# RWKV heads: the inverse's blocks doubled by products of 32 and 64 rows in place of masked products of 128

## The chip, the cores and the metric

The kernel runs on one core of a Trainium2 chip. The number that counts is the time of one execution on the device, in microseconds (us). Before the change the median of 3 runs is 2561.5 us, with 2560.05 and 2563.88 us as the lowest and the highest. Five engines of the core work side by side, each on its own queue: TensorE (PE, with its weight loads as PEld), VectorE (DVE), ScalarE (ACT), GpSimd (POOL) and SyncE (SP), which issues most of the transfers.

## What is computed

Two blocks follow each other on 256 tokens of width 2048. The second begins with an RWKV group of 16 heads of width 64, beside an attention group. The part of the reference that the change touches is the recurrence of a head:

```python
def step(state, inp):
    r_t, w_t, k_t, v_t, kk_t, a_t = inp
    sa = jnp.einsum('bhvk,bhk->bhv', state, -kk_t)
    state = (state * w_t[:, :, None, :]
             + sa[..., None] * (kk_t * a_t)[:, :, None, :]
             + v_t[..., None] * k_t[:, :, None, :])
    return state, jnp.einsum('bhvk,bhk->bhv', state, r_t)
```

The kernel does not step through the tokens. It takes the 256 tokens as two chunks of 128 and solves the recurrence of a chunk by the inverse of a triangular 128 x 128 matrix per head, one plus a strictly triangular matrix of scores.

## The kernel before

**Halves, chunks and head groups.** `rwkv_half(hf, ...)` does 8 heads at a time, for `hf` = 0 and 1. Inside it `heads4(hg)` takes a group of 4 heads, `hg` = 0 and 1, and goes through the two chunks, `t` = 0 and 1; the second chunk needs the state `s0` that the first leaves. `together` takes the two groups in turns, one `yield` each, so what follows comes twice in the program at each place: four times over `hf` and `t`, each with two groups of 4 heads.

**The inverse.** The scores `sa` are made first. The 32 x 32 blocks on the diagonal of all 16 matrices of a half are inverted together on VectorE, one row after another (lines 1408 to 1412, tile `inv`), then turned into `invt` and `invx`, two layouts of one inverse (lines 1417 and 1418). Then `heads4` spreads the four blocks of each of its heads over a 128 x 128 matrix with zeros beside them (`spread`, line 1433), once as `wt` and once as its transpose `xt`, and doubles the blocks twice, from 32 to 64 (`l` = 5) and from 64 to 128 (`l` = 6). Each doubling is a product of the scores with `xt` (`pz`, line 1451), a multiplication with a mask `lev` that keeps the blocks beside the diagonal pairs (`zt`, line 1453), a product with `wt` (`pw`, line 1457) and an addition to `wt` (line 1458). Before the second doubling `xt` is made anew by a transpose on TensorE (`px`, line 1445) and a copy on ScalarE (line 1447). All of these are whole 128 x 128 matrices, 4 to a tile of 512 columns.

**What stands around it.** After the doubling come `pk` (line 1462) with `rhs` (1464), the product with the inverse `pg` (1471) and its copy `ga` (1473), the scores `psr` with `sr` (1389, 1391), and the output `py` (1489, 1490). At `t` = 0 the new state `pst` follows (1501, 1502), with 8 copies `s` on ScalarE (1508). At `t` = 1 the correction of the state, `rh` (1484), comes in before `py`. After both chunks the output `y` is normalised (1525 to 1543), mostly on VectorE.

**The other work.** `project` streams weights: SP loads `wr` (line 159), ScalarE rounds it into `wh` (148), VectorE makes the rest `wl` (151, 154), and TensorE does three products of 512 columns each (lines 163 to 165). The order in which each engine gets its instructions is laid down when the program is built, by a scheduler that goes by data and buffers. In half 0 it has placed products of the next projections between the steps of `heads4`; in half 1 there are none, and the chains of the two groups stand alone. The tag `side` has 3 banks of PSUM, in which `pz`, `pw`, `px`, `pk`, `pg`, `psr` and `py` follow one another.

Of the kernel before, what the change touches and what calls it, by code (L numbers as in the profile page):

```python
# [12 lines left out]
AL = mybir.AluOpType  # L13
# [11 lines left out]
C_IDENT, C_LT, C_GT, C_ONES, C_BD32, C_LE, C_SEL2, C_SEL4, C_FREQ, C_SEL8, C_ID32, C_ALL = (  # L25
    0, 128, 256, 384, 512, 640, 768, 770, 772, 796, 828, 860)
# [28 lines left out]
def tile_kernel(ctx: ExitStack, tc: tile.TileContext, I: dict, out: bass.AP):  # L55
    nc = tc.nc
    V, S, G, PE = nc.vector, nc.scalar, nc.gpsimd, nc.tensor
# [25 lines left out]
    def tl(tag, shape=None, dt=F, name=None):  # L83
        pool, (n, bufs) = (sb, BASE[tag]) if tag in BASE else (phase[1], phase[2][tag])
        shape = [128, n] if shape is None else shape
        return pool.tile(shape, dt, name=name or tag, tag=tag, bufs=bufs)
# [4 lines left out]
    def psum(tag, shape=None, name=None):  # L91
        return phase[3].tile(shape or [128, 512], F, name=name or tag, tag=tag, bufs=phase[4][tag])
# [4 lines left out]
    def pside(shape=None, name="side"):  # L97
        return psum("side", shape, name)
# [4 lines left out]
    def const(shape, name, dt=F):  # L103
        return sb.tile(shape, dt, name=name, bufs=1)
# [3 lines left out]
    cst = const([128, C_ALL], "cst")  # L108
    nc.sync.dma_start(cst[:, :128], I["cst"][:, :128])
    ident = cst[:, C_IDENT:C_IDENT + 128]  # L110
# [361 lines left out]
    for g in range(4):  # L472
        m = tl("g", [128, 2, 512], name="mem")
# [92 lines left out]
    lev = const([128, 7 * 128], "lev", U8)  # L566
# [39 lines left out]
    for d in range(2):  # L606
        for half in range(2):
            w = gate_w(d, half)
            la = []
            for t in range(2):  # L610
                px = pside()
# [18 lines left out]
            for q in (0, 2):  # L630
                pst = pside([128, 2, 256], name="pst")
                for r in range(2):
                    h = half * 2 + (q + r) // 2
# [261 lines left out]
    for p in range(2):  # L895
# [12 lines left out]
        for q in (0, 2):  # L908
            pt = transpose2(lambda t, kt: of[:, t, kt * 128:(kt + 1) * 128], q)
            h, l = ybT.h[p][:, q:q + 2], ybT.l[p][:, q:q + 2]  # L910
# [296 lines left out]
    bc4 = lambda m: m[:, None, :].to_broadcast([128, 4, 128])  # L1207
# [61 lines left out]
    def rwkv_half(hf, kx, rx, vx):  # L1269
# [6 lines left out]
        for dst, p0, b0 in ((sgm, 0, W0), (av, 64, A0)):  # L1276
            for q in (0, 2):
                pd = pside([128, 2, T], name="pd")
                for r in range(2):
                    PE.matmul(pd[:, r], wup[p0:p0 + 64, (q + r) * 128:(q + r + 1) * 128], lora[p0:p0 + 64, 0],  # L1280
                              start=True, stop=True)
                for r in range(2):
                    c = b0 + hf * 4 + q + r
# [19 lines left out]
        for q in (0, 2):  # L1303
            sq = tl("m", [128, 2, T], name="ksq")
            S.activation(sq, kk[:, q:q + 2], AF.Square)
            for r in range(2):
                c = C_SEL8 + (q + r) * 8
# [20 lines left out]
        for q in (0, 2):  # L1328
            fa = tl("m", [128, 2, T], name="fa")
            for r in range(2):  # L1330
                c = hf * 4 + q + r
# [3 lines left out]
            for r in range(2):  # L1335
                c = RK + hf * 4 + q + r
                V.scalar_tensor_tensor(qq[:, r], rx[:, q + r], pr3[:, c:c + 1], kx[:, q + r], op0=AL.mult, op1=AL.mult)
                c = C_SEL8 + (q + r) * 8
# [60 lines left out]
        for t in range(2):  # L1399
            for hg in range(2):  # L1400
                sa = sas[t, hg] = tl("g" if hf else "xt", [128, 2, 2, 2, 128], name="sa")
                scores(lambda o: sa[:, o], kk, strict, hg, t, "sa")
                b0 = (t * 2 + hg) * 4
# [12 lines left out]
        invx = tl("g", [128, 32, 32], name="invx")  # L1416
# [5 lines left out]
        def heads4(hg):  # L1422
            s0 = None
            for t in range(2):
# [3 lines left out]
                nt_ = lambda i: sa[:, i % 2, 0, i // 2]  # L1428
                b0 = (t * 2 + hg) * 4

                def spread(x, name):
                    d = tl("m", [128, 4, 128], name=name)
                    V.tensor_tensor(wide(d), x[:, :, b0:b0 + 4].rearrange("p i h -> p h i")[:, :, None, :].to_broadcast([128, 4, 4, 32]),
                                    wide(bc4(cst[:, C_BD32:C_BD32 + 128])), op=AL.mult)
                    return d


                wt = spread(invt, "wt")
                xt = spread(invx, "xt")
                for l in range(5, 7):  # L1440
                    yield
                    if l == 6:
                        px = pside([128, 4, 128], name="px")
                        for i in range(4):
                            PE.transpose(px[:, i], wt[:, i], ident)
                        xt = tl("m", [128, 4, 128], name="xt")
                        S.copy(xt, px)
                        yield
                    pz = pside([128, 4, 128], name="pz")
                    for i in range(4):  # L1450
                        PE.matmul(pz[:, i], nt_(i), xt[:, i], start=True, stop=True)  # L1451
                    zt = tl("m", [128, 4, 128], name="zt")
                    V.tensor_tensor(zt, pz, bc4(lev[:, l * 128:(l + 1) * 128]), op=AL.mult)
                    yield
                    pw = pside([128, 4, 128], name="pw")
                    for i in range(4):
                        PE.matmul(pw[:, i], zt[:, i], wt[:, i], start=True, stop=True)  # L1457
                    V.tensor_tensor(wt, pw, wt, op=AL.add)
                yield
                pk = pside([128, 4, 64], name="pk")  # L1460
                for i in range(4):
# [15 lines left out]
                if t:  # L1477
                    yield
                    pr_ = pside([128, 2, 128], name="pr_")
                    for i in range(4):  # L1480
                        c, o = divmod(i, 2)
# [5 lines left out]
                for i in range(4):  # L1487
                    c, o = divmod(i, 2)
                    PE.matmul(py[:, i], sr[o][:, 0, c], ga[:, i, :64], start=True, stop=False)
                    PE.matmul(py[:, i], sr[o][:, 1, c], vn[:, t, hg * 256 + i * 64:hg * 256 + i * 64 + 64], start=False,  # L1490
                              stop=t == 0)
# [3 lines left out]
                if t == 0:  # L1495
                    yield
                    pst = pside([128, 2, 64], name="pst")
                    for i in range(4):
                        c, o = divmod(i, 2)
# [10 lines left out]
        for _ in together(*[heads4(hg) for hg in range(2)]):  # L1510
            pass
# [221 lines left out]
    for hf in range(2):  # L1733
        for q in (0, 2):
            pt = transpose2(lambda t, kt: yr[hf][:, t, kt * 128:(kt + 1) * 128], q)
            h, l = yrT.h[hf][:, q:q + 2], yrT.l[hf][:, q:q + 2]
# [176 lines left out]
```

## Time and profile before

| | us |
|---|---|
| median of 3 runs | 2561.5 |
| lowest, highest | 2560.05, 2563.88 |
| the profiled execution | 2557.92 |
| its span in the trace | 2556.2 |
| PE busy in it | 2422.8 (95%) |
| DVE busy | 1796.2 (70%) |
| ACT busy | 1170.2 (46%) |

An engine counts as busy from the start of an instruction to its end, and those of TensorE overlap: a row of several products counts the whole stretch. The granted clock is given as a share of full speed, 1.00 for 2.4 GHz and 0.50 for 1.2 GHz. In the timeline a row may merge several instructions of one line (x16); each f32 product of the program leaves two records there, for `pz` 128 records for 64 products.

### The profile page before, as it was taken

To read this page: it belongs to the slowest core of one execution; us is meant where nothing else is said; L and a number is where in the kernel's file an instruction comes from. 1 tells how busy PE (TensorE), PEld (TensorE's weight loads), DVE (VectorE), ACT (ScalarE), POOL (GpSimd) and SP (SyncE) were. 2 spreads that over 40 slices of the span, in tenths; PEclk is the share of its full clock that TensorE was granted. 3 is DMA by queue.
4 is the path that set the end of the run, shared out by engine and by line. 5 is a ranking of instruction groups with operands and counts; after the bars stand their busy time and mean duration, and the time that the engine had idled before them with its cause. 6 is when DMAs were issued, how large, how long until landed. Compare 5 with 4: busy or idle time off the path is not lost.

```text
span 2556.2 us, 32427 instructions
## 1 busy us (share of the span) xinstructions
PE 2422.8 (95%) x11491; PEld 1928.6 (75%) x11491; DVE 1796.2 (70%) x2991; ACT 1170.2 (46%) x1560; POOL 172.1 (7%) x169
## 2 busy tenths in 40 slices
PE   8999998889989998998999999999999999999998
PEld 5667766778767776787878677787888888888886
DVE  5898657997897888967687978755655544555544
ACT  6543244444653544445642452445544433444433
POOL 0000010220230010002020120100000000000000
PEclk9999999999999999999999999999999999999999
DMA  7877547676656788755633243145466555666554
GB/s 262 276 251 225 170 153 242 218 232 228 198 183 218 233 282 288 259 182 158 198 94 110 80 136 99 63 163 192 133 189 182 186 187 187 189 184 187 201 188 154
DMA packets 267358, 483.11 MB, mean 189 GB/s; under 512 B 21137, under 2 KB 45547, under 8 KB 267195
## 3 DMA queue, kind: packets, MB, share of 16 engines
q1 hardware_dynamic: 266875, 480.60, 58.4%
q8 instruction: 90, 1.47, 0.2%
q14 instruction: 73, 0.60, 0.1%
q10 hardware_dynamic: 320, 0.44, 0.1%
HBM read 477.82 MB, written 3.15 MB: 188 GB/s over the span
## 4 chain that ended last, share of the span: by engine, by line
PE 61%; DVE 18%; DMA 11%; issue 6%; ACT 3%; POOL 1%; SPq 0%; DVEq 0%; ACTq 0%; POOLq 0%
PE acc L165 17%; PE acc L164 17%; PE acc L163 17%; DMA ar<-in_w_ada 8%; DVE wl L154 6%; DVE aa L405 3%; PE trp L236 2%; ACT wh L148 1%; DMA lnb<-in_ln_b 1%; PE pw L1457 1%; PE pz L1451 1%; DVE u L1411 1%; DVE inv L1412 1%; DMA wr<-in_w_in_e 1%; DMA wr<-in_w_in_o 0%
## 5 line engine op out<-in xcount | busy, mean ns | idle before, releaser
L148 ACT CAST wh<-wr 128x1024 fp32r<-128x1024 f32 (+2 forms) x736 | 760.3, 1038 | 991.6 <-PE acc L165 804.6
L164 PE MATMUL acc<-wl,xh 128*128 128x512 f32 (+2 forms) x2560 | 1005.5, 393 | 22.9 <-DVE wl L154 22.7
L163 PE MATMUL acc<-wh,xh 128*128 128x512 f32 (+2 forms) x2560 | 1011.8, 396 | 14.1 <-ACT xh L253 6.1
L165 PE MATMUL acc<-wh,xl 128*128 128x512 f32 (+2 forms) x2560 | 1003.5, 393 | 2.4 <-DVE xl L254 1.9
L154 DVE TENSOR_TENSOR wl<-wr,wh 128x512 fp32r<-128x512 f32 (+2 forms) x928 | 622.3, 702 | 176.8 <-ACT wh L148 176.1
L164 PEld LDWEIGHTS acc<-wl,xh 128*128 128x128 f32 x2560 | 485.1, 189 | 135.8 <-DVE wl L154 37.2
L151 DVE TENSOR_TENSOR wl<-wr,wh 128x1024 fp32r<-128x1024 f32 x272 | 333.3, 1225 | 357.4 <-ACT wh L148 355.4
L163 PEld LDWEIGHTS acc<-wh,xh 128*128 128x128 f32 x2560 | 484.6, 189 | 127.1 <-ACT wh L148 10.0
L165 PEld LDWEIGHTS acc<-wh,xl 128*128 128x128 f32 x2560 | 484.8, 189 | 106.3 <-issue 4.0
L405 DVE SCALAR_TENSOR_TENSOR aa<-ar,cs,aa 128x512 f32<-128x512 f32 x240 | 191.0, 796 | 72.8 <-DMA ar<-in_w_ada 71.5
L165 PE MATMUL acc<-wh,ucl 128*128 128x512 f32 x128 | 50.9, 398 | 0.0
L164 PE MATMUL acc<-wl,uch 128*128 128x512 f32 x128 | 50.7, 396 | 0.0
L163 PE MATMUL acc<-wh,uch 128*128 128x512 f32 x128 | 49.8, 389 | 0.0
L381 DVE SCALAR_TENSOR_TENSOR am<-ar,cs,am 128x512 f32<-128x512 f32 x60 | 42.6, 746 | 7.3 <-DMA ar<-in_w_ada 7.3
L722 PE MATMUL pp<-eq,ek 128*128 128x128 f32 x224 | 29.4, 286 | 6.1 <-DVE ek L734 6.1
L722 PEld LDWEIGHTS pp<-eq,ek 128*128 128x128 f32 x224 | 28.5, 201 | 8.4 <-issue 5.0
L1055 POOL TENSOR_TENSOR sgo<-sgo,psc 128x512 f32<-128x512 f32 x8 | 14.6, 1850 | 295.5 <-ACT sgo L1049 164.8
L350 PE MATMUL ada<-wl,c 128*4 128x512 f32 x64 | 26.0, 406 | 4.2 <-DVE wl L154 4.2
L164 PE MATMUL acc<-wl,dh 128*128 128x512 f32 x64 | 26.2, 410 | 3.8 <-DVE wl L154 3.7
L457 DVE SCALAR_TENSOR_TENSOR xl<-trp,pr,xh 128x256 fp32r<-128x256 f32 x48 | 22.3, 480 | 10.1 <-ACT xh L456 9.9
L1866 ACT ACTIVATE un<-acc,rml 128x512 f32<-128x512 f32 x32 | 22.0, 689 | 15.6 <-PE acc L165 15.6
L163 PEld LDWEIGHTS acc<-wh,uch 128*128 128x128 f32 x128 | 24.4, 191 | 5.6
(592 smaller groups left out, 2457.3 us busy)
## 6 DMA issues: line engine op xcount, KB each, us to landing
ar<-in_w_ada SPq DMA_DIRECT2D x288, 256.0 KB
wr<-in_w_in_e SPq DMA_DIRECT2D x128, 512.0 KB
wr<-in_w_up SPq DMA_DIRECT2D x128, 512.0 KB
wr<-in_w_down SPq DMA_DIRECT2D x128, 512.0 KB
wr<-in_w_in SPq DMA_DIRECT2D x80, 512.0 KB
wr<-in_w_in_o SPq DMA_DIRECT2D x64, 512.0 KB
wr<-in_w_ada SPq DMA_DIRECT2D x64, 256.0 KB
wr<-in_w_out_e SPq DMA_DIRECT2D x32, 512.0 KB
```

The costliest lines, as they stand in the source:

```text
L148: S.copy(wh, wr)
L151: engines[0].tensor_tensor(wl, wr, wh.bitcast(F), op=AL.subtract)
L154: engines[q % 2].tensor_tensor(wl[:, q], wr[:, q], wh[:, q].bitcast(F), op=AL.subtract)
L163: PE.matmul(acc, xh, wh, start=start, stop=False)
L164: PE.matmul(acc, xh, wl, start=False, stop=False)
L165: PE.matmul(acc, xl, wh, start=False, stop=stop)
L236: PE.transpose(pt[:, q, t * 128:(t + 1) * 128], src(t, kt + q), ident)
L350: PE.matmul(acc, c4[:, k0 + q], wl[:, q], start=False, stop=k0 + q == 15)
L381: V.scalar_tensor_tensor(acc[a], w[:, q], col, acc[a], op0=AL.mult, op1=AL.add)
L405: V.scalar_tensor_tensor(acc, w, cs[:, k:k + 1], acc, op0=AL.mult, op1=AL.add)
L722: PE.matmul(pp[:, h, t], kx[:, 2 * h + c, s * 128:(s + 1) * 128], qx[:, 2 * h + c, t * 128:(t + 1) * 128], start=c == 0, stop=c == 1)
L1411: V.tensor_tensor(u, inv[:, j + 1:, j:j + 1].to_broadcast([128, n, j]), inv[:, j:j + 1, :j].to_broadcast([128, n, j]), op=AL.mult)
```

## The change

`xt` as a whole matrix, the masks, the additions and the transpose `px` go. The first doubling takes the 32 x 32 blocks: `pz` multiplies the scores' block beside a diagonal pair with the block of `invx` itself, for the blocks 0 and 2 (8 products of 32 x 32 for 4 heads). The two results are copied to `zt` by VectorE and by ScalarE. `pw` then makes the two blocks beside the diagonal (8 products), which ScalarE copies into `wt`, and a third product for the transposed upper pair, which VectorE copies into `x6`, a 64 x 64 layout of the first pair that VectorE has spread from `invx`. The second doubling takes one block of 64 x 64 per head: `pzz` (4 products), a copy by VectorE (`zzt`), `pww` (4 products) and a copy by ScalarE into `wt`. That is 28 small products for 4 heads in place of 16 products and 4 transposes of 128 x 128.

```diff
@@ -1436,26 +1436,40 @@
 
 
                 wt = spread(invt, "wt")
-                xt = spread(invx, "xt")
-                for l in range(5, 7):
-                    yield
-                    if l == 6:
-                        px = pside([128, 4, 128], name="px")
-                        for i in range(4):
-                            PE.transpose(px[:, i], wt[:, i], ident)
-                        xt = tl("m", [128, 4, 128], name="xt")
-                        S.copy(xt, px)
-                        yield
-                    pz = pside([128, 4, 128], name="pz")
-                    for i in range(4):
-                        PE.matmul(pz[:, i], nt_(i), xt[:, i], start=True, stop=True)
-                    zt = tl("m", [128, 4, 128], name="zt")
-                    V.tensor_tensor(zt, pz, bc4(lev[:, l * 128:(l + 1) * 128]), op=AL.mult)
-                    yield
-                    pw = pside([128, 4, 128], name="pw")
-                    for i in range(4):
-                        PE.matmul(pw[:, i], zt[:, i], wt[:, i], start=True, stop=True)
-                    V.tensor_tensor(wt, pw, wt, op=AL.add)
+                x6 = tl("m", [128, 4, 64], name="x6")
+                V.tensor_tensor(x6[:64].rearrange("p h (g c) -> p h g c", c=32),
+                                invx[:64, :, b0:b0 + 4].rearrange("p i h -> p h i")[:, :, None, :].to_broadcast([64, 4, 2, 32]),
+                                cst[:64, C_BD32:C_BD32 + 64].rearrange("p (g c) -> p g c", c=32)[:, None].to_broadcast([64, 4, 2, 32]),
+                                op=AL.mult)
+                rows32 = [slice(g * 32, g * 32 + 32) for g in range(4)]
+                pz = pside([128, 4, 32], name="pz")
+                for i in range(4):
+                    for g in (0, 2):
+                        PE.matmul(pz[rows32[g + 1], i], nt_(i)[rows32[g], rows32[g + 1]], invx[rows32[g], :, b0 + i],
+                                  start=True, stop=True)
+                zt = tl("m", [128, 4, 32], name="zt")
+                for g in (1, 3):
+                    (V.tensor_copy if g == 1 else S.copy)(zt[rows32[g]], pz[rows32[g]])
+                yield
+                pw = pside([128, 2, 4, 32], name="pw")
+                for i in range(4):
+                    for g in (0, 2):
+                        PE.matmul(pw[rows32[g], 0, i], zt[rows32[g + 1], i], wt[rows32[g + 1], i, rows32[g + 1]], start=True, stop=True)
+                    PE.matmul(pw[rows32[1], 1, i], wt[rows32[1], i, rows32[1]], zt[rows32[1], i], start=True, stop=True)
+                V.tensor_copy(x6[rows32[1], :, :32], pw[rows32[1], 1])
+                for g in (0, 2):
+                    S.copy(wt[rows32[g], :, rows32[g + 1]], pw[rows32[g], 0])
+                yield
+                pz = pside([128, 4, 64], name="pzz")
+                for i in range(4):
+                    PE.matmul(pz[64:, i], nt_(i)[:64, 64:], x6[:64, i], start=True, stop=True)
+                zt = tl("m", [128, 4, 64], name="zzt")
+                V.tensor_copy(zt[64:], pz[64:])
+                yield
+                pw = pside([128, 4, 64], name="pww")
+                for i in range(4):
+                    PE.matmul(pw[:64, i], zt[64:, i], wt[64:, i, 64:], start=True, stop=True)
+                S.copy(wt[:64, :, 64:], pw[:64])
                 yield
                 pk = pside([128, 4, 64], name="pk")
                 for i in range(4):
```

The lines behind the change stand 14 higher: `pk` is line 1476, `rhs` 1478, `pg` 1485, `ga` 1487, `s` 1522.

VectorE, half 1, first chunk, from the turned inverse to `rhs`; before, `wt` and `xt` for each of the two groups stand first:

```order
L1418 STREAM_TRANSPOSE invx<-inv 128x1024
L1433 TENSOR_TENSOR wt<-invt,cst 128x512
L1433 TENSOR_TENSOR xt<-invx,cst 128x512
L1433 TENSOR_TENSOR wt<-invt,cst 128x512
L1433 TENSOR_TENSOR xt<-invx,cst 128x512
L1453 TENSOR_TENSOR zt<-pz,lev 128x512 x2
L1458 TENSOR_TENSOR wt<-pw,wt 128x512 x2
L1453 TENSOR_TENSOR zt<-pz,lev 128x512 x2
L1458 TENSOR_TENSOR wt<-pw,wt 128x512 x2
L1464 COPY rhs<-pk 128x4x64 x2
```

And now (`x_13077` and `x_13093` are `x6` of the two groups):

```order
L1418 STREAM_TRANSPOSE invx<-inv 128x1024
L1433 TENSOR_TENSOR wt<-invt,cst 128x512
L1440 TENSOR_TENSOR x_13077<-invx,cst 64x256
L1452 COPY zt<-pz 32x128
L1433 TENSOR_TENSOR wt<-invt,cst 128x512
L1440 TENSOR_TENSOR x_13093<-invx,cst 64x256
L1452 COPY zt<-pz 32x128
L1459 COPY x_13077<-pw 32x4x32
L1459 COPY x_13093<-pw 32x4x32
L1467 COPY zzt<-pzz 64x256 x2
L1478 COPY rhs<-pk 128x4x64 x2
```

The second group's `wt` now stands behind the first group's `zt`, which waits for TensorE, and eight multiplications or additions of 512 columns have become six copies of 128 or 256.

ScalarE, half 1, from the end of the first chunk into the second (`s_13202`, `s_13221` and later `s_13250`, `s_13281` are the states of the two groups). Before:

```order
L1473 COPY ga<-pg 128x4x64 x2
L1494 COPY y<-py 128x256 x2
L1508 ACTIVATE s_13202<-pst,fs 64x64 x4
L1508 ACTIVATE s_13221<-pst,fs 64x64 x4
L1447 COPY xt<-px 128x512 x2
L1473 COPY ga<-pg 128x512 x2
```

And now:

```order
L1487 COPY ga<-pg 128x4x64 x2
L1508 COPY y<-py 128x256 x2
L1522 ACTIVATE s_13250<-pst,fs 64x64 x4
L1452 COPY zt<-pz 32x128
L1522 ACTIVATE s_13281<-pst,fs 64x64 x4
L1452 COPY zt<-pz 32x128
L1461 COPY wt<-pw 32x4x32 x4
L1472 COPY wt<-pww 64x4x64 x2
L1487 COPY ga<-pg 128x512 x2
```

ScalarE's share of the first doubling stands behind the states of the first chunk. Each of its copies of `zt` also waits for VectorE's copy of the same tile.

TensorE, half 0, first chunk, the second doubling among the products of a projection. Before:

```order
L1445 MATMUL px<-cst,wt 128x128 x8
L163 MATMUL acc<-wh,xh 128x512
L164 MATMUL acc<-wl,xh 128x512
L165 MATMUL acc<-wh,xl 128x512
L1451 MATMUL pz<-xt,sa 128x128 x8
L1457 MATMUL pw<-wt,zt 128x128 x8
L1462 MATMUL pk<-vn,sa 128x64 x8
```

And now (`x_11030` and `x_11046` are `x6`):

```order
L1465 MATMUL pzz<-x_11030,sa 64x64 x4
L165 MATMUL acc<-wh,xl 128x512
L163 MATMUL acc<-wh,xh 128x512
L1465 MATMUL pzz<-x_11046,sa 64x64 x4
L164 MATMUL acc<-wl,xh 128x512
L165 MATMUL acc<-wh,xl 128x512
L1471 MATMUL pww<-wt,zzt 64x64 x8
L1476 MATMUL pk<-vn,sa 128x64 x8
```

Products of 512 columns now stand between small ones at more places. From the first `pz` to `pk` there were 9 of them in the first chunk and, from `pst` on, 5 in the second; now there are 12 and 9. In half 1 none stands there, before or after. SP's and POOL's queues keep their order.

## Rows read from the trace of the kernel before

**Rows 1.** The page, busy time and chain: engine, us, share, instructions.

```profile
PE 2422.8 (95%) x11491; PEld 1928.6 (75%) x11491; DVE 1796.2 (70%) x2991; ACT 1170.2 (46%) x1560; POOL 172.1 (7%) x169
PE acc L165 17%; PE acc L164 17%; PE acc L163 17%; DMA ar<-in_w_ada 8%; DVE wl L154 6%; DVE aa L405 3%; PE trp L236 2%; ACT wh L148 1%; DMA lnb<-in_ln_b 1%; PE pw L1457 1%; PE pz L1451 1%; DVE u L1411 1%; DVE inv L1412 1%; DMA wr<-in_w_in_e 1%; DMA wr<-in_w_in_o 0%
```

**Rows 2.** Windows around half 1: length, PE, PEld, DVE, ACT, POOL busy, PEclk, DMA.

```profile
1570.00:1580.00 10.00, 6.01 (x33) 5.87 (x34) 7.79 (x9) 0.00 (x0) 0.00 (x0) 0.66 0.12 45
1580.00:1590.00 10.00, 9.76 (x92) 9.41 (x92) 4.31 (x7) 1.92 (x4) 0.00 (x0) 1.00 0.00 0
1640.00:1660.00 20.00, 19.71 (x118) 16.38 (x117) 14.86 (x42) 12.96 (x30) 0.00 (x0) 1.00 0.44 146
```

**Rows 3.** Timeline, half 1, first chunk: start us, us, engine, line, operation.

```profile
1570.16 1.86 DVE L1418 STREAM_TRANSPOSE invx<-inv 128x1024 f32<-128x1024 f32 x1
1571.95 0.97 DVE L1433 TENSOR_TENSOR wt<-invt,cst 128x512 f32<-128x512 f32 x1
...
1573.99 3.91 PE L1451 MATMUL pz<-xt,sa 128*128 128x128 f32 x16 [4.89 <-DVE xt L1433]
...
1585.13 1.90 PE L1462 MATMUL pk<-vn,sa 128*128 128x64 f32 x16
```

**Rows 4.** Timeline, half 1, second chunk.

```profile
1595.56 0.34 PE L1501 MATMUL pst<-ga,bn 128*64 128x64 f32 x4
...
1596.39 2.57 ACT L1508 ACTIVATE s<-pst,fs 64x64 f32<-64x64 f32 x8 [0.35 <-PE pst L1502]
...
1606.30 1.90 PE L1462 MATMUL pk<-vn,sa 128*128 128x64 f32 x16
```

**Rows 5.** Timeline, half 0, both chunks.

```profile
1359.40 2.00 DVE L1418 STREAM_TRANSPOSE invx<-inv 128x1024 f32<-128x1024 f32 x1
...
1375.63 1.90 PE L1462 MATMUL pk<-vn,sa 128*128 128x64 f32 x16
...
1386.75 0.34 PE L1501 MATMUL pst<-ga,bn 128*64 128x64 f32 x4
...
1398.07 1.90 PE L1462 MATMUL pk<-vn,sa 128*128 128x64 f32 x16
```

**Rows 6.** Timeline, half 1: weight loads of products of several shapes, and two copies on VectorE.

```profile
1581.24 1.92 PEld L1451 LDWEIGHTS pz<-xt,sa 128*128 128x128 f32 x16
...
1586.17 0.42 DVE L1464 COPY rhs<-pk 128x256 f32<-128x256 f32 x1
...
1588.74 0.52 PEld L1389 LDWEIGHTS psr<-rr,av 64*128 64x128 f32 x8
...
1589.18 0.53 PEld L1389 LDWEIGHTS psr<-rr,rk 64*128 64x128 f32 x8
...
1594.96 0.30 PEld L1489 LDWEIGHTS py<-ga,sr 128*128 128x128 f32 x2
...
1595.18 0.30 PEld L1490 LDWEIGHTS py<-vn,sr 128*128 128x128 f32 x2
...
1595.55 0.20 PEld L1501 LDWEIGHTS pst<-ga,bn 128*64 128x64 f32 x4
...
1596.37 0.25 PEld L1502 LDWEIGHTS pst<-vn,kn 128*64 128x64 f32 x4
...
1598.49 0.16 DVE L1526 TENSOR_SCALAR ymean<-ymean 128x8 f32<-128x8 f32 x1
```

**Rows 7.** Timeline, a projection ahead of half 1.

```profile
1563.09 0.39 PE L165 MATMUL acc<-wh,xl 128*128 128x512 f32 x1
...
1563.54 0.39 PE L164 MATMUL acc<-wl,xh 128*128 128x512 f32 x1
```

**Rows 8.** Windows of 1 and 2 us, columns as in rows 2: where the clock was low.

```profile
158.00:159.00 1.00, 1.00 (x8) 0.88 (x7) 0.95 (x4) 0.34 (x1) 0.00 (x0) 0.77 0.85 319
1576.00:1578.00 2.00, 2.00 (x11) 2.00 (x11) 0.75 (x2) 0.00 (x0) 0.00 (x0) 0.50 0.00 0
1580.00:1582.00 2.00, 1.76 (x15) 1.51 (x15) 0.69 (x1) 1.03 (x2) 0.00 (x0) 1.00 0.00 0
```

**Rows 9.** Timeline of TensorE just ahead of the first window of rows 8.

```profile
157.26 1.15 PE L356 MATMUL pm<-cst,m 4*128 4x128 f32 x8 [0.79 <-DVE m L353]
158.34 0.97 PE L236 MATMUL trp<-cst,xn 128*128 128x128 f32 x4
```

## The prediction

> **What bounds the kernel now.** I read the page first. TensorE is busy for 95% of the span, and the chain that ended last runs 17% each through the three products of the projections; the doublings `pz` and `pw` stand in it with 1% each, some 50 us together [rows 1]. So the kernel as a whole is bound by TensorE's projections, and the question is what bounds the four stretches in which the inverses are doubled. The windows around half 1 tell that: no transfer to speak of from 1570 us on, VectorE busy for 4.3 us of 10 and ScalarE for 1.9 [rows 2]. TensorE counts 9.8 of 10, but no projection stands there: it works through the chain's own products, one stage after the other, each handed to VectorE and back. Whatever shortens a stage there shortens the whole. From 1640 us on TensorE is full again with projections [rows 2] and stays so; its work there does not change, so time saved in a chain is not given back later.
>
> I measure each chain to the first `pk`, since everything from there on is as before. In half 1 the first chunk's chain starts when VectorE ends `invx`, at 1570.16 + 1.86 = 1572.02, and `pk` starts at 1585.13: 13.1 us [rows 3]. For the second chunk I count from the first `pst`, 1595.56, to `pk` at 1606.30: 10.7 us [rows 4]. In half 0 it is 1361.40 to 1375.63, 14.2 us, and 1386.75 to 1398.07, 11.3 us [rows 5]; 9 and 5 products of projections stand in these two.
>
> **Prices.** A copy on VectorE took 0.42 us for 256 columns, an operation on 8 columns 0.16 [rows 6]; on that line 128 columns cost 0.29. The spread `wt` of 512 columns took 0.97 [rows 3], so `x6` with half the columns should take 0.5. An activation on ScalarE took 2.57/8 = 0.32 [rows 4]; I take that for each of its small copies. A product of 512 columns takes (1563.54 - 1563.09)/2 = 0.225 us [rows 7].
>
> No row shows a product of 32 x 32. Its price is bounded by the nearest ones. Each f32 product leaves two records. With weights of 128 columns a record takes 1.92/16 = 0.12 us; `psr`, with 64 rows, 0.44/8 = 0.055; `pst`, with weights of 64 columns, (1596.37 - 1595.55)/28 = 0.029 [rows 6]. So 0.029 to 0.12; nearest by shape is `pst`, then `psr`, and I take 0.04. A change of shape costs something too: from `py` to `pst` it is 0.37 us from load to load, where it is 0.22 from one pair of `py` to the next: 0.15 us [rows 6].
>
> This last row has a rule beside it. The Trainium skill, TensorEngine Tiling, section Key Properties, says that changing the tiling mode, not merely the tile, drains TensorE. The trace agrees with 0.15 us at the change from `py` to `pst`; were such changes free, as if that rule did not hold, the saving below would be 2.7 us larger.
>
> **The new chain, first chunk of half 1.** `pz` no longer waits for the spreads; it runs on `invx` itself while VectorE does `wt`, `x6`, `zt`, then the same for the second group: 2 x (0.97 + 0.5 + 0.29) = 3.5 us. `pz` (32 records, 1.3 us) and the first group's `pw` (24 records, 1.0 us) lie beside it. ScalarE's copy of the second `zt` waits for VectorE's: 0.32. Then on the path: `pw` of the second group, 24 records, `pzz` and `pww`, 8 each: 40 x 0.04 = 1.6; the copy to `x6` 0.3 and to `zzt` 0.42; the tail of the last record twice, 0.2 each, 0.4; five hand-overs of some 0.06 (an estimate), 0.3; two changes of shape (32 to 64, 64 to 128), 0.3. ScalarE's copies into `wt` lie beside `pzz`, and the last one beside `pk`, which hides it. Sum 3.52 + 0.32 + 3.32 = 7.2, against 13.1: 5.9 us less at full clock.
>
> **The clock.** At 1576 us TensorE runs at 0.50 of full speed, after standing idle while VectorE turned and spread the inverse; it is back at 1.00 in the window from 1580 [rows 8], after the dense 128-wide `pz` and `pw`. Now these are gone, and TensorE waits for most of the chain. I assume that the low clock lasts through the chain and into `pk` and `pg` behind it, and take 2.0 off: 40 records at twice the price are 1.6, the rest is for `pk`. The other end is 3.4, if `pk` and `pg` (3.7 us together) run low as well, or 0. **First chunk of half 1: 3.9 us less.**
>
> **Second chunk of half 1.** What is late here is ScalarE: its copies of `zt` stand behind the states of the first chunk. From `pst`: 16 records and a tail, 0.7; four activations, 1.3; `zt`, 0.32; four more, 1.3; `zt`, 0.32: 3.9 us, where VectorE's spreads and the mean of `y`, which now stand between its copies, are ready in time. Behind that the same as above, 40 records and so on: 3.3. Sum 7.2 against 10.7: **3.5 us less**. TensorE comes from dense `py` here, and I charge no low clock; the other end is 3.4.
>
> **Half 0.** The same two chains, with products of projections among them. First chunk: 7.2, plus 12 products, 2.7 us, of which half fills waits of the chain, 1.35; one `wl` on VectorE that stands before the second copy to `x6`, 0.68; ten changes of shape more, 1.5, half of them in waits, 0.75. Sum 10.0 against 14.2, and 3 products more than before are then done, 0.7: **4.9 us less**. Second chunk: 7.2 + 1.0 for half of 9 products + 0.75 = 9.0 against 11.3, and 4 products more, 0.9: **3.2 us less**.
>
> **Sum.** 3.9 + 3.5 + 4.9 + 3.2 = 15.5 us. The profiled execution would go from 2557.92 to 2542.4. It lies 3.6 below the median of the runs; the difference holds for the median, 2561.5 - 15.5 = 2546. The bounds: with records at 0.029 (1.8 more), no loss by the clock (2.0) and all products and changes of shape hidden (3.85), 23.2 us; with 0.055 (2.4 less), nothing hidden (3.85) and the low clock to its other ends (1.4 and 3.4), 4.5 us. What I count at nothing is VectorE's lighter work beyond the path (six small copies for eight operations of 512 columns): it has idle time in these chains. The changed order of other work around half 0's end I charge at nothing too, since the same instructions follow there.
>
> **The rivals.**
>
> *Small products are as dear as large ones.* The change makes 28 products of 16 products and 4 transposes. If a small record costs what a wide one does, 0.12 [rows 6], the chain goes by TensorE: 56 records of `pz` and the first `pw` with 0.5 of waits, 40 more behind, 1.7 of the rest: 13.7 us. The four chains then take 54.8 + 1.35 + 0.68 + 0.75 + 1.0 + 0.75 = 59.3 us against 49.3 + 1.6 for the products done meanwhile: 8.4 us more, 2570 us. It decides from 0.1 us per record on, where the chains are even. For it: both blocks of a `pz` go to one bank, where `psr` has a bank for each of its halves. Against it: `pst` writes one bank with two column groups at 0.029 [rows 6]. The Trainium skill, TensorEngine Tiling, section Gotcha 1: PSUM Pressure, says that different row tiles cannot access one PSUM bank at the same time; no row shows two row tiles at one bank, and by that rule the blocks 0 and 2 would take turns and a record would lie nearer to 0.055. Chance 7%.
>
> *The low clock takes it.* Ahead of 158 us TensorE was busy with products that use 4 rows of the array, and the granted clock was 0.77 of full speed right behind them [rows 8, 9]: products that fill little of the array may not keep it up. If each chain ends at half speed and leaves `pk` and what follows low for 3.4 us or more in half 1, with the dear ends of the other terms, about 4.5 us remain: 2557, within what can be told from no change. Chance 10%.
>
> *Half 0 gives nothing.* There TensorE always has projections to do [rows 5], and if the chain's idle time was filled anyway only half 1 counts: 7.4 us, 2554. Against it: TensorE's own work falls, from 72 wide records a pair of groups (8.6 us) to 112 small ones (4.5). Chance 12%.
>
> *More than forecast*: PE's waits vanish as the bound says and more, below 2538. Chance 5%.
>
> **How the numbers follow.** My forecast, 10 to 23 us less, has 66%; with half 0 giving nothing 12% and the larger gain 5%, faster by more than 0.2% (5.1 us, about what a measurement of this kernel tells from no change) has 83%; the low clock is the 10% for no change, the dear products the 7% for slower. The range from 2538 to 2557 takes in the bounds of 23.2 and 4.5 us, and leaves out the slower case, the larger gain and half of the low clock.
>
> **What would show it.** In the profile after, `pk` of half 1 should start some 9 us after `invx` ends and 7.2 us after the first `pst`. The loads of `pz` and `pw` should follow each other by 0.03 to 0.055 us. ScalarE's `zt` should follow the states, and TensorE's granted clock between `invx` and `pk` tells the second rival. I am wrong if a small record takes 0.1 us or more, if the second chunk waits for something else than ScalarE, or if the time from the end of the chains to the end of the kernel has grown.

## The result, and the profile after

The change makes the kernel slower: 2574.64 us as the median of 6 runs against 2562.69 for the kernel before beside it, a ratio of 1.0053 with a 95% interval of 1.0037 to 1.007. That is 12 us more, where I forecast 15.5 us less. In a later comparison the ratio was 1.0046 (last experiment). The profiled execution took 2572.85 us, its span is 2571.1.

Here is the page of the changed kernel, busy time by engine. TensorE has 160 more records of products and is busy 18 us longer than in [rows 1], though the products it got are smaller than those it lost.

```profile
PE 2441.1 (95%) x11651; PEld 1943.4 (76%) x11651; DVE 1777.4 (69%) x2983; ACT 1174.7 (46%) x1584; POOL 171.0 (7%) x169
```

The timeline of half 1 of the changed kernel, start and duration in us, from the turned inverse to the first `py` of the second chunk. It answers to [rows 3, 4].

```profile
1579.30 1.86 DVE L1418 STREAM_TRANSPOSE invx<-inv 128x1024 f32<-128x1024 f32 x1
...
1581.28 0.99 PEld L1448 LDWEIGHTS pz<-invx,sa 32*32 32x32 f32 x32 [3.48 <-issue]
...
1587.26 1.84 PEld L1471 LDWEIGHTS pww<-wt,zzt 64*64 64x64 f32 x16
...
1589.22 3.67 PE L1476 MATMUL pk<-vn,sa 128*128 128x64 f32 x16
1592.69 3.62 PE L1485 MATMUL pg<-rhs,wt 128*128 128x64 f32 x16
...
1608.11 0.49 PE L1515 MATMUL pst<-ga,bn 128*64 128x64 f32 x4
...
1609.39 1.27 ACT L1522 ACTIVATE s<-pst,fs 64x64 f32<-64x64 f32 x4 [0.80 <-PE pst L1516]
1610.68 0.26 ACT L1452 COPY zt<-pz 32x128 f32<-32x128 f32 x1
...
1616.83 3.67 PE L1476 MATMUL pk<-vn,sa 128*128 128x64 f32 x16
1620.29 3.73 PE L1485 MATMUL pg<-rhs,wt 128*128 128x128 f32 x16
...
1629.34 0.43 PE L1503 MATMUL py<-ga,sr 128*128 128x64 f32 x2
```

Read the starts. From the end of `invx` (1581.16) to `pk` it is 8.1 us, 13.1 before: the chain that the change shortens did get shorter. The 16 records of `pk`, untouched by the change, take 3.67 us in place of 1.90, and from `pk` to `pst` it is 18.9 us. The same rows of half 0, which answer to [rows 5]:

```profile
1361.58 1.90 DVE L1418 STREAM_TRANSPOSE invx<-inv 128x1024 f32<-128x1024 f32 x1
...
1375.64 3.67 PE L1476 MATMUL pk<-vn,sa 128*128 128x64 f32 x16
1379.07 0.77 PE L163 MATMUL acc<-wh,xh 128*128 128x512 f32 x1
1379.65 0.63 PE L164 MATMUL acc<-wl,xh 128*128 128x512 f32 x1
...
1396.24 0.49 PE L1515 MATMUL pst<-ga,bn 128*64 128x64 f32 x4
...
1405.89 2.00 PE L1476 MATMUL pk<-vn,sa 128*128 128x64 f32 x16
...
1416.23 0.43 PE L1503 MATMUL py<-ga,sr 128*128 128x64 f32 x2
```

Two rows of the kernel before close the comparison at the far end, the first `py` of the second chunk in half 0 and in half 1:

```profile
1407.85 0.43 PE L1489 MATMUL py<-ga,sr 128*128 128x64 f32 x2
...
1614.89 0.43 PE L1489 MATMUL py<-ga,sr 128*128 128x64 f32 x2
```

From these rows and [rows 3, 4, 5], each piece before and after, in us:

| piece | half 0 before | after | half 1 before | after |
|---|---|---|---|---|
| end of `invx` to `pk`, t = 0 | 14.2 | 12.2 | 13.1 | 8.1 |
| `pk` to `pst`, t = 0 | 11.1 | 20.6 | 10.4 | 18.9 |
| `pst` to `pk`, t = 1 | 11.3 | 9.7 | 10.7 | 8.7 |
| `pk` to `py`, t = 1 | 9.8 | 10.3 | 8.6 | 12.5 |

The four doubling chains became 10.8 us shorter together. What stands behind them, in which the change touches no instruction of the heads, became 22.4 us longer; in half 0 the order puts 11 products of projections there where there were 8, at 0.225 us each [rows 7] some 0.7 us of it. The balance is 11.6 us more, and the medians differ by 12. (The two profiled spans differ by 14.9; the other 3.3 us lie outside these stretches and are no more than executions of one kernel differ among themselves.)

The windows of the changed kernel say why. The columns are as in [rows 2]: length, busy time of PE, PEld, DVE, ACT, POOL, then the granted clock. First half 0, then half 1.

```profile
1366.00:1368.00 2.00, 2.00 (x25) 1.40 (x26) 1.73 (x5) 0.60 (x3) 0.00 (x0) 0.50 0.00 0
1384.00:1386.00 2.00, 2.00 (x18) 2.00 (x18) 0.00 (x0) 0.37 (x1) 0.00 (x0) 0.50 0.04 15
1398.00:1400.00 2.00, 2.00 (x18) 1.41 (x18) 1.93 (x3) 1.80 (x7) 0.45 (x1) 0.54 0.00 0
1400.00:1402.00 2.00, 2.00 (x53) 1.27 (x55) 1.23 (x5) 1.22 (x5) 0.40 (x1) 1.00 0.00 0
...
1580.00:1582.00 2.00, 0.69 (x25) 0.72 (x27) 2.00 (x3) 0.00 (x0) 0.00 (x0) 0.68 0.21 80
...
1590.00:1592.00 2.00, 2.00 (x11) 2.00 (x11) 0.42 (x1) 0.00 (x0) 0.00 (x0) 0.50 0.00 0
...
1618.00:1620.00 2.00, 2.00 (x11) 2.00 (x11) 0.42 (x1) 0.00 (x0) 0.00 (x0) 0.50 0.00 0
...
1624.00:1626.00 2.00, 2.00 (x22) 2.00 (x22) 0.32 (x1) 0.58 (x1) 0.00 (x0) 0.72 0.29 107
```

TensorE goes at half speed (1.2 in place of 2.4 GHz) from about 1366 to 1399 us and from about 1581 to 1625 us: 33 and 44 us, busy in most of the windows. In half 0 products of projections with 512 columns stand among the chain's own in this time, three in a row from 1379.07 us on (two of them are shown above), and the clock stays at 0.50 through them. In the kernel before it was back before `pk` in both halves, in half 1 by [rows 8]; for half 0 these are its windows, which I had not read:

```profile
1363.00:1365.00 2.00, 1.71 (x9) 1.72 (x9) 2.00 (x3) 0.00 (x0) 0.00 (x0) 0.61 0.01 3
1365.00:1367.00 2.00, 2.00 (x12) 1.95 (x10) 1.29 (x3) 0.00 (x0) 0.00 (x0) 0.54 0.00 0
1367.00:1369.00 2.00, 2.00 (x18) 1.91 (x17) 1.77 (x3) 0.00 (x0) 0.00 (x0) 1.00 0.00 0
```

### The profile page after: what moved, and what is told of

It is laid out like the page before. It is cut to its first block, busy times and chain, and to the rows that moved or that the text cites. A ratio compares the mean times of both kernels' runs of the same rounds, so it can differ in the third digit from the quotient of the medians.

```text
span 2571.1 us, 32754 instructions
## 1 busy us (share of the span) xinstructions
PE 2441.1 (95%) x11651; PEld 1943.4 (76%) x11651; DVE 1777.4 (69%) x2983; ACT 1174.7 (46%) x1584; POOL 171.0 (7%) x169
## 4 chain that ended last, share of the span: by engine, by line
PE 66%; DVE 16%; DMA 10%; issue 4%; ACT 3%; POOL 1%; SPq 0%; DVEq 0%; ACTq 0%; POOLq 0%
PE acc L165 18%; PE acc L164 18%; PE acc L163 18%; DMA ar<-in_w_ada 7%; DVE wl L154 5%; DVE aa L405 2%; PE trp L236 2%; ACT wh L148 1%; DMA wr<-in_w_in_o 1%; PE psr L1389 1%; DVE u L1411 1%; DVE inv L1412 1%; PE pk L1476 0%; DMA lnb<-in_ln_b 0%; PE pg L1485 0%
## 5 line engine op out<-in xcount | busy, mean ns | idle before, releaser
L163 PEld LDWEIGHTS acc<-wh,xh 128*128 128x128 f32 x2560 | 486.0, 190 | 128.7 <-ACT wh L148 11.3
L1055 POOL TENSOR_TENSOR sgo<-sgo,psc 128x512 f32<-128x512 f32 x8 | 13.9, 1752 | 293.1 <-ACT sgo L1049 164.8
```

The source lines that it names most:

```text
L163: PE.matmul(acc, xh, wh, start=start, stop=False)
```

## The experiments

Theory 1: the masked 128 x 128 products of the old doublings brought the clock back on their way; without them it stays low through `pk`, `pg`, `psr` and `py`, and that costs more than the chains gain. Theory 2, the rival: the small products, their hand-overs and their order are dear in themselves, and the clock is a bystander. Added products write to a tile of the tag `bg`, not to the three banks of `side`, and nothing reads it. The edits are shown shortened, some of them in words.

**One doubling of each kind.** The first run keeps the small first doubling and makes the second as before (transposes, product, mask, product, 128 wide); the second run the other way round.

```diff
 e1: first doubling small, then
-  pzz, zzt, pww of 64 rows
+  px (4 transposes), xt, pz 128x128, zt masked, pw 128x128, wt += pw
 e2: first doubling masked 128x128, then
+  px (4 transposes of 64x64), x6
   pzz, zzt, pww of 64 rows
```

> Only the first doubling is small; the second is the old round of masked 128x128 products (transposes, product, mask, product). Theory 1 (the clock): the time was lost because, after the idle time behind the transposed inverse, nothing but products of few moving columns follows and the clock stays at 0.50 through pk, pg, psr and py (pk to pst 20.6 us in half 0 and 18.9 us in half 1, before 11.1 and 10.4). The 12 dense 128-column products in front of pk bring it back: pk's 16 records about 1.9 to 2.5 us in place of 3.7, pk to pst 11 to 13 us at t = 0 in both halves, and the kernel about 2556 to 2563. Theory 2 (the small products and their hand-overs are dear in themselves): half of them is left, so about half of the 12 us lost, 2566 to 2570, with pk at 3.7 us as in the changed kernel.

> Only the second doubling is small (its transposed operand by four 64x64 transposes); the first is the old round of masked products. Theory 1: the 8 dense products come first, then 12 small ones with waits between them; the clock comes back partly, and falls or stays according to which comes last, so 2558 to 2568; pk's 16 records take 1.9 us where the granted clock is 1.00 in front of them and 3.7 us where it is 0.50, and the time of the kernel goes with that and not with the number of small products. Theory 2: about half of the loss, 2566 to 2570, whatever the clock.

Measured: 0.9988 of before (0.9971 to 1.0005) for the small first doubling, 1.0003 (0.9984 to 1.0022) for the small second. By the ratios the small first doubling alone is 17 us faster than both (1.0053 - 0.9988 of 2560): far more than the half of the loss that theory 2 gives back. The interval of the small second doubling reaches up to 1.0022, into that half, so its time alone does not decide. The stretches do: `pk` to `pst` is 11.1 and 10.4 us in one, 11.0 and 10.5 in the other, as before the change. Two rows of the first run, half 1:

```profile
1575.09 1.90 PE L1476 MATMUL pk<-vn,sa 128*128 128x64 f32 x16
...
1585.51 0.34 PE L1515 MATMUL pst<-ga,bn 128*64 128x64 f32 x4
```

The second run has more to show. In its half 1 the clock is at 1.00 behind the first chunk and then falls behind `pzz` and `pww` of the second chunk. Its TensorE timeline and its windows there:

```profile
1596.92 1.25 PE L1461 MATMUL pzz<-x,sa 64*64 64x64 f32 x16
1598.11 1.28 PE L1467 MATMUL pww<-wt,zzt 64*64 64x64 f32 x16
1599.33 3.67 PE L1472 MATMUL pk<-vn,sa 128*128 128x64 f32 x16
```

```profile
1596.00:1597.00 1.00, 0.56 (x8) 0.34 (x6) 0.52 (x1) 0.37 (x1) 0.00 (x0) 1.00 0.00 0
1597.00:1598.00 1.00, 1.00 (x16) 0.96 (x16) 0.37 (x1) 0.37 (x1) 0.00 (x0) 1.00 0.00 0
1598.00:1599.00 1.00, 1.00 (x16) 0.88 (x15) 0.48 (x2) 0.18 (x1) 0.00 (x0) 1.00 0.00 0
1599.00:1600.00 1.00, 1.00 (x10) 0.90 (x8) 0.00 (x0) 0.56 (x2) 0.00 (x0) 0.60 0.00 0
```

TensorE has hardly stood idle ahead of this fall: 0.44 us in the window from 1596 and, from 1587 us on, 0.14 us besides. From 1597 on it is busy throughout, with products of 64 x 64, and loses the clock all the same. `pk` takes 3.67 us, and from `pk` to `py` it is 11.9 us (8.6 before).

**The clock given back by extra products.** A burst ahead of `pk`, and products in the waits.

```diff
 e3, behind pww of the second group, t = 0
+  12 products of 512 columns
 e4, t = 0
+  2 f32 products of 512 columns on invt, ahead of the first pz
+  3 products of 512 columns behind pz, each pw, each pzz and the last pww
```

> The changed kernel with 12 extra products of 512 moving columns, whose results nothing uses, between the last small product and pk at t = 0 of both halves. Theory 1: they bring the clock back: pk 1.9 us, pk to pst 11 to 12 us (20.6 and 18.9 without); they cost 2.7 us each time at full clock, at most 5.4 us at 0.50, so the kernel gains 18 less 5 to 11: 2562 to 2569. Theory 2: pure extra work in the chain, 2575 plus 5 to 11: 2580 to 2586.

> The changed kernel with extra products of 512 moving columns, whose results nothing uses, put at t = 0 of both halves into the waits that TensorE has there anyway: 2 behind the transposed inverse in front of the first small product, 3 in each wait for a copy of a small product. Theory 1: the clock is back before pk at little cost, since TensorE was idle there: pk to pst 10.5 to 12 us in both halves, the chain ahead of pk at most 2 to 3 us longer: 2553 to 2562. Theory 2: the clock at pk changes nothing that matters: 2575 to 2582.

Measured: 1.0014 (0.9998 to 1.003) and 0.9978 (0.9956 to 1.0001). Both give TensorE further products and are, by the ratios, faster than the changed kernel by 10 and 19 us. Theory 2 called for 5 to 11 us more in the first and for no gain in the second, and it falls here. In the run with a burst `pk` to `pst` is back to 10.8 and 10.4 us. In the run with products in the waits the clock is 1.00 throughout half 0 and the first chunk of half 1. Its rows, half 1:

```profile
1570.82 1.14 PE L1487 MATMUL pww<-wt,zzt 64*64 64x64 f32 x16
1571.89 0.96 PE L1430 MATMUL warm<-xh 128*128 128x512 f32 x3
1572.68 1.89 PE L1494 MATMUL pk<-vn,sa 128*128 128x64 f32 x16
...
1590.47 3.67 PE L1494 MATMUL pk<-vn,sa 128*128 128x64 f32 x16
```

The first `pk` takes 1.89 us. The second, at t = 1, where no product was added, takes 3.67: the clock fell there too.

**Only the columns of `pk` and `pg`.** No product is added or moved; `pk`, and `pg` at t = 0, get their 64 moving columns twice.

```diff
-  PE.matmul(pk[:, i], sa[...], vn[:, t, h], ...)
+  PE.matmul(pk[:, i].rearrange("p (a b) -> p a b", a=2), sa[...],
+            vn[:, t, h][:, None, :].to_broadcast([128, 2, 64]), ...)
```

> The changed kernel with the same 64 moving columns given twice to pk, and to pg at t = 0, so that these products have 128 moving columns (the second 64 columns of the result are not used); no other product is added. Reading 1a (the clock came back in the kernel before because its products there had 128 moving columns, and stays away because pk and pg have 64): the clock returns within pk and pg of t = 0, psr and py go at full clock, pk to pst 15 to 17 us in place of 20.6 and 18.9, and the kernel 2562 to 2570. Reading 1b (the columns don't matter; the pauses ahead do): the clock stays at 0.50 to py as in the changed kernel, pk to pst 19 to 21 us, the kernel 2572 to 2578.

Measured: 0.9969 (0.9949 to 0.9988), some 21 us below the changed kernel and beyond what reading 1a called for. The timeline and the windows of half 1:

```profile
1576.12 3.78 PE L1476 MATMUL pk<-vn,sa 128*128 128x128 f32 x16
1579.69 2.10 PE L1489 MATMUL pg<-rhs,wt 128*128 128x128 f32 x16
...
1588.45 0.34 PE L1520 MATMUL pst<-ga,bn 128*64 128x64 f32 x4
```

```profile
1576.00:1578.00 2.00, 2.00 (x11) 1.88 (x10) 0.00 (x0) 0.37 (x1) 0.00 (x0) 0.50 0.03 8
1578.00:1580.00 2.00, 2.00 (x11) 2.00 (x11) 0.42 (x1) 0.00 (x0) 0.00 (x0) 0.50 0.00 0
1580.00:1582.00 2.00, 2.00 (x20) 1.88 (x21) 0.42 (x1) 0.55 (x2) 0.00 (x0) 1.00 0.00 0
```

`pk` starts at 0.50 as in the changed kernel and takes 3.78 us with twice the columns (3.67 with 64): at half speed these cost next to nothing. Then the clock is back, `pg` takes 2.10 us in place of 3.62, and `pk` to `pst` is 12.3 us (18.9). In half 0 it is 12.6 (20.6). TensorE was as busy by the profile in one as in the other; the columns of `pk` and `pg` are what the edit changes. The control is the same edit in the kernel before:

> The kernel before, with its full masked products, and the same wide pk and pg (128 moving columns at t = 0): the control for the changed kernel with wide pk and pg, which was 0.9969 of before. If those gain by the clock alone, there is nothing to gain here, since the clock is at 1.00 from before pk on: 2556 to 2562, ratio 0.999 to 1.001 (each set of 16 records is 0.05 to 0.15 us longer). If the wide products are a gain in themselves, 0.992 to 0.997.

Measured: 0.9992 (0.9974 to 1.0011). Where the clock is already up, the wide products gain nothing that can be told. So their gain in the changed kernel is the clock's.

**Extra products alone, fewer, and more.** Four f32 products in the old kernel's wait ahead of its first `pz`; the two of that place alone in the changed kernel; and the products in the waits also at t = 1 of half 1.

```diff
 e6 (kernel before) and e8 (changed kernel), behind invt
+  for _ in range(4):    # 2 in e8
+      PE.matmul(bank, ident, flat(invt)[:, :512], ...)
 e7 (as the products in the waits)
-  if t == 0 and hg in ...
+  if (t == 0 or hf) and hg in ...
```

> The kernel before, with its full masked products, and 4 extra products of 512 moving columns behind the transposed inverse, in the wait in front of the first pz (results not used). It tells how much of the gain of the small products with extra products in the waits is theirs, and how much the extra products alone give. Theory 1 (the clock decides, and at equal clock the small products are worth the 3 to 6 us per half that their shorter chains show): the first pz in half 1 goes at 2.2 us in place of 3.9, the chain to pk is about 3 us shorter, nothing else moves; 1 to 4 us faster than before, and 3 to 6 us slower than the small products with extra products in the waits. Theory 2 (the small products are worth nothing, the extra products all): as fast as those, about 0.998 of before or under.

> The changed kernel with only the 2 extra products of 512 moving columns behind the transposed inverse, in front of the first small product, and none in the waits between the small products. If the long pause in front (3.1 us in half 1) is what takes the clock, it holds through the small products and pk is 1.9 us: 2555 to 2562. If the pauses between the small products and their few columns take it, it falls before pk, pk is 3.7 us again, and the kernel stays at 2568 to 2576.

> The small products with extra products in the waits at t = 0 of both halves, as measured, and the same also in the waits at t = 1 of half 1, where the clock fell to 0.50 from pk to psr (pk 3.67 us, pst to py 18.8 us). Theory 1: the clock stays at 1.00 there, pk 1.9 us, pst to py 15 to 16.5 us, so 2 to 4 us less than without: 0.996 to 0.997 of before. Theory 2: extra products in a chain that has no room for them, 1 to 4 us more than without.

The old kernel with extra products: 1.0016 (1.0002 to 1.003), 4 us slower where I expected 1 to 4 faster. The clock is at 1.00 in both halves, and the stretches from the start of `invx` to the first `py` of the second chunk are 1.4 and 0.9 us shorter (theory 1 had some 3 in half 1), so the low clock cost the old kernel little there. But from that `py` of half 0 to the start of `invx` of half 1 it is 4.3 us longer (166.6 against 162.3). TensorE has projections to do there, and the added 3.7 us of products may push these back; that is not shown, and this stretch is 160.7 to 164.8 us in the other traces. Theory 2's reading, that the extra products are the whole gain of the small products with them, finds no support: 1.0016 here, 0.9978 there, though the two runs do not add the same products.

Two products in front alone: 1.0004 (0.9981 to 1.0027). Half 0 has the clock at 1.00 throughout, and `pk` to `pst` is 11.4 us. In half 1, where no projections stand between the small products, it lasts only into the waits:

```profile
1564.00:1566.00 2.00, 0.68 (x24) 0.46 (x24) 1.94 (x4) 0.26 (x1) 0.00 (x0) 1.00 0.00 0
1566.00:1568.00 2.00, 1.62 (x31) 1.44 (x32) 0.78 (x4) 1.08 (x5) 0.00 (x0) 0.57 0.00 0
1572.00:1574.00 2.00, 2.00 (x11) 2.00 (x11) 0.42 (x1) 0.00 (x0) 0.00 (x0) 0.50 0.00 0
```

There `pk` to `pst` is 18.9 us again. So both of my answers were half right: in half 0 the pause in front decides, in half 1 the small products and their pauses do.

Products at t = 1 as well: 0.9978 (0.9965 to 0.9991), the same as without them. The clock is 1.00 through the second chunk of half 1, and `pk` to `py` there falls from 11.4 to 8.5 us; but `pst` to `pk` grows from 7.4 to 11.0, with the 18 added products in the chain itself. My 2 to 4 us less were a miss: what the clock gives is spent again.

**A version that beats both.** The wide `pk` and `pg`, and the two products in front in half 0 alone; and then the 64 x 64 products widened as well.

```diff
 e9
+  wide pk, pg as above
+  if not hf: the 2 products behind invt
 e10: e9, and
-  pzz, pww with 64 moving columns
+  pzz, pww with the same 64 moving columns twice
```

> The changed kernel with pk and pg on 128 moving columns (as measured, the clock comes back within pk at t = 0 of half 0, but was at 0.50 for 14 us ahead of that), and in half 0 alone the 2 extra products in front of the first small product, which held the clock at 1.00 throughout half 0 when they stood alone. Half 1 as with the wide products alone. If the two gains add, the stretch from the transposed inverse to the first py of t = 1 is 42 us in half 0 (45.1 with the wide products alone, 48.5 in the kernel before) and 40.7 in half 1 (44.7 before): 8 to 10 us under the kernel before, ratio 0.996 to 0.997. If half 0 has other work that ends last, its shorter stretch moves nothing: ratio 0.997 to 0.9985.

> As the kernel before it in this call, and the 64x64 products of the second doubling also get their moving columns twice (128 in place of 64). If moving columns bring the clock back whatever the stationary operand's size, it returns in half 1 already within these products or at pk's start, about 2 us sooner at t = 0 and t = 1: up to 3 us less. If wide columns cost more than that in these small products (16 records of each of the two, now 0.11 us apiece at the low clock), up to 2 us more.

Measured: 0.9962 (0.9945 to 0.9979) and 0.9981 (0.9962 to 1.0001). The first has the lowest ratio of all here (its interval overlaps that of the wide products alone), about 10 us below the kernel before and, by 0.9962 / 1.0053, 0.9% below the changed one. Its stretches from the start of `invx` to the first `py` of the second chunk are 40.9 and 40.0 us, before 48.4 and 44.7. The second is 4 us slower by the medians, with intervals that overlap. Its half 1, TensorE's timeline and windows:

```profile
1572.02 2.98 PE L1475 MATMUL pww<-wt,zzt 64*64 64x128 f32 x13
1574.93 3.78 PE L1480 MATMUL pk<-vn,sa 128*128 128x128 f32 x16
```

```profile
1570.00:1572.00 2.00, 2.00 (x15) 2.00 (x14) 0.43 (x1) 0.00 (x0) 0.00 (x0) 0.50 0.04 8
1574.00:1576.00 2.00, 2.00 (x10) 1.67 (x9) 0.00 (x0) 0.36 (x1) 0.00 (x0) 0.50 0.00 0
1578.00:1580.00 2.00, 2.00 (x16) 2.00 (x15) 0.42 (x1) 0.17 (x1) 0.00 (x0) 0.78 0.00 0
```

A record of `pww` now takes about 0.22 us, where it took 0.115 at the same clock, and the clock still comes back only within `pk`. Twice the columns in these products of 64 x 64 did not bring the clock back.

**The changed kernel again**, beside the control.

> The changed kernel once more, beside the control: 1.0053 of before as first measured, with the clock at 0.50 through pk, pg, psr and py of t = 0 in both halves. If the loss was of the chip of the first comparison, 1.000 or under.

Measured: 1.0046 (1.0027 to 1.0066). The loss was not one of the first comparison alone. In this execution the low clock of half 0 lasted to about 1414 us, through the second chunk as well, so how long it lasts varies between executions of one kernel (33 us in half 0 above, 51 here).

## Why the prediction was wrong

**What bounds the stretches** was right for this change: the chains' own stages, one after another. The four stretches grew by 11.6 us, the medians by 12. It was not so in the old kernel with extra products, whose stretches are 2.3 us shorter and whose time is 4 us longer.

**Prices and chains** were right, or nearly. A record of `pz` took 0.99/32 = 0.031 us even at half speed; I took 0.04. The Trainium skill, TensorEngine Tiling (Array Packing), section Gotcha 1: PSUM Pressure, says that different row tiles cannot access one PSUM bank at the same time; by that the blocks 0 and 2 would have taken turns. No turn that costs time shows: 0.031 lies by the 0.029 of `pst`, not by 0.055. The 64 x 64 records I had too cheap: 0.067 at full clock (1570.82 to 1571.89 for 16) and 0.115 at half, against 0.04, and all 16 of `pww` stand in a row ahead of `pk`, where I counted 8. At full clock the chains were 10.2 us (half 0, t = 0, with two products in front alone), 8.4 (t = 1) and 7.4 (half 1, t = 1, products in the waits), where I had 10.0, 9.0 and 7.2; half 1, t = 0 was 8.1 at half speed, where I had 9.2. ScalarE's `zt` does stand behind the states, at 1610.68, as forecast. By these rows the chains would have been worth about the 15.5 us.

**The clock** is the step that failed. I charged 2.0 us, with 3.4 as the other end, in one of four chains, and 3.4 as the bound in a second; measured, what stands behind the four chains grew by 22.4 us. The other end was also added up wrong: 1.6 for the 40 records at twice the price and 3.7 more for `pk` and `pg` make 5.3, not 3.4. Three choices were wrong in it. First, I let the low clock end within `pk` and `pg` at the latest. In the kernel before it had ended behind the dense `pz`, which has 128 moving columns; `pk` and `pg` have 64 at t = 0, and no row showed that they bring it back. They did not, and given 128 columns they did. Second, I charged nothing in half 0, where products of projections stand among the chain: I had not read the granted clock there, and its rows show 0.54 at 1365 us, in the kernel before already. Third, I charged nothing at t = 1, where TensorE "comes from dense `py`": the second chunk of half 1 starts at 0.50 in the changed kernel, and in the runs of the small products that had the clock back at t = 0 of that half it falls to 0.50 again, but for the one with products in the waits at t = 1 too.

**The rivals.** *The low clock takes it* was the right mechanism, with a 10% chance; of the 11 us that it takes off, the clock's own part is 6.8, 3.4 in each chain of half 1, where the stretches behind the chains lost 22.4. It charged half 0 nothing and counted 3.4 us for `pk` and all that follows, so it ended at no change and not on the slower side. The row that it rested on, 0.77 behind 158 us, has 0.79 us of idle time ahead of its products on 4 rows [rows 9], so it does not tell the products from the pause. *Small products dear* is excluded by the 0.031 us, by the 0.067 at full clock and by the runs with extra products. *Half 0 gives nothing* was wrong as it was put: its chains are 3.7 us shorter, and what stands behind them is 10.0 us longer.

**What would make it wrong**: I named a longer time behind the chains, and that is what came. I also named a small record of 0.1 us or more. The 64 x 64 records reached that at half speed, with 0.115, where a wide record took 3.91/16 = 0.24 [rows 3]; at full clock they took 0.067.

## What to carry to other kernels

Ask of each product that a change removes whether it was also what brought TensorE's clock back behind a pause, and read the granted clock in every stretch that the change touches, through to the first later place where it rises. A low clock is priced by all the work up to there, not by the chain that is changed. Where f32 products with few moving columns stand at a low clock, try to give them the same columns twice: here it took 21 us off a kernel, for 0.1 us in each set of 16 records.

## What the runs showed of the hardware

- TensorE stayed at 0.50 for 33 and 44 us in the changed kernel, through windows in which it was busy 2.00 of 2.00 us.
- In the rises read here TensorE had just done products on 128 rows and 128 columns of weights with 128 moving columns or more: the masked `pz`, the wide `pk`, `pg` at t = 1, or products of 512 columns. Products of 512 columns were no sure way back: three in a row from 1379.07 us on in half 0 of the changed kernel went by at 0.50, and of the twelve ahead of `pk` nearly all did in half 0 and about six in half 1. In the changed kernel it did not rise in `pk`, `pg`, `psr` and `py` of t = 0, nor, with twice the columns, in the 64 x 64 products of half 1. The runs don't tell these apart any further.
- It fell also where TensorE had hardly stood idle: behind `pzz` and `pww` of 64 x 64, with 0.58 us of idle time in the 12 us ahead of the fall (1587 to 1599).
- At half speed an f32 record on weights of 128 x 128 takes nearly the same with 64 moving columns as with 128: 3.67 and 3.78 us for 16.
- A 32 x 32 f32 record takes 0.031 us at half speed (0.99 for 32) and 0.029 at full clock (0.93 for 32, products in the waits).
